# Hybrid attention and convolution step on one core: mixer weights moved to ScalarE's DMA queue, and the convolution's end rewritten

## The chip, the cores and the metric

The kernel runs on one core of a Trainium2 chip. The time is the device time of one execution, in microseconds (us), lower being better. TensorE is written PE, VectorE DVE, ScalarE ACT, GpSimd POOL and SyncE SP, as the profile writes them. The chip runs each engine's instructions in their own order; an instruction that waits holds up what stands behind it on its engine.

## The reference, cut to what matters

One layer of a decoder trunk for 528 prompt tokens (512 and 16 learned ones) and 32 sample tokens (8 sequences of 4), D = 1024, all in float32:

```
h = h + 0.5 * swiglu(rmsnorm(h, ffn1_norm), ffn1_w_gate, ffn1_w_up, ffn1_w_down)
n = rmsnorm(h, mix_norm)
q_lat, q_rope, c_kv, k_rope, glu = project_mixers(n, pos, w_in, q_norm, w_uq, kv_norm, w_uk)
a = attn_fn(q_lat, q_rope, c_kv, k_rope, w_uv)
cv, conv_state = conformer_conv(glu, conv_prev, conv_w, conv_b, conv_ln_g, conv_ln_b)
mix = jnp.concatenate([rmsnorm(a, attn_grp_norm), rmsnorm(cv, conv_grp_norm)], axis=-1) @ w_out
h = h + mix
h = h + 0.5 * swiglu(rmsnorm(h, ffn2_norm), ffn2_w_gate, ffn2_w_up, ffn2_w_down)
```

`conformer_conv` is a causal depthwise convolution of width 31 over 512 channels, then a LayerNorm over the channels and a swish. The sample tokens attend to 4096 cached latent rows each, which lie in pages of 128 rows x 256 columns behind a page table; the prompt attends to itself. After the layer comes a last RMSNorm.

## The kernel before, in words

Tensors lie with channels on the partitions and tokens along the free dimension. The program has three stretches: the first feed-forward part, the mixers (from about 400 to 736 us of the span), and the second feed-forward part with the last norm.

**Weights.** Every float32 weight block of 128x512 (256 KB) is loaded into a `wr` tile (3 of them) by `w_dma` (the DMA is L284, issued by SP), then split by `w_split` into a rounded part `wh` (ACT, L302) and the rest `wl` (POOL, L304). A product takes three matmuls: wh with the high and with the low part of the data, wl with the high part. When block j has been split, the load of block j + 3 is issued; it waits until POOL has read the `wr` tile three blocks back. The mixers' blocks are those of w_in (24), w_r (1), w_uq (4), w_uk (2), w_uv (2) and w_out (16), and `mixers` holds their indices.

**Sample attention.** 32 chunks run one after another, 16 for each of two groups. `load_chunk` issues 8 page DMAs of 256 KB (L1036, SP; tile slots "w" where the chunk's number divides by 3 and is at most LAST_W, otherwise "y", 8 slots, which is two chunks) and 2 indirect DMAs (L1023, POOL). `chunk_scores` gives `sc` (L1070), `chunk_pt` transposes the softmax's numerators into `pts` (L1079, L1081 on ACT), and `chunk_pv` multiplies them with the page (`ob`, L1092); after chunk LAST_W it sets `w_free`, upon which the residual `h` is loaded back (L1588) into the "w" slots.

**Prompt attention.** 16 units in two workers give `s` (L1261), `pr` (L1277), `pts` (L1302), `po` (L1317) and fill `at`.

**Convolution.** `conv_proc` runs 31 taps for each of four channel blocks on DVE (L942) into `acc`. `conv_tail` takes the mean (`mu`), squares the four blocks into four temporaries `sq` of the pool "t", sums the squares over the channels with `rsqrt` (L452, 4 matmuls per block into one PSUM tile `p1`), forms 1/sqrt (L484 is a square root on ACT that needs a table load of its own; L485 to L488 are on DVE), spreads it over the partitions (`spread`, L503 to L507), applies the LayerNorm, the tanh (`th`, L981) and the swish, and does the same again for conv_grp_norm. `scaled` (L900) then writes a temporary `cg`, and `split` (L905 ACT, L906 POOL) makes `conv_out[ct]` of it in a slot of "x" or "z". "z" has 5 slots: two hold the convolution's result `acc2`, two the attention's result `at`.

**The end of the mixers.** `attn_norm` waits for all units and the sample's end, squares `at`, sums, scales in place (L900) and splits into `mix_a` (L905 ACT, L906 DVE), and then gives both slots of `at` back. main() waits for `conv_done` and `w_free`, runs `out_half(conv_out)` eight times (12 matmuls for each half of the tokens, L371) and adds into `h` (L1582); then it waits for the attention's norm and does the same for `mix_a`.

**Order.** The program is written by generators that a planner of its own steps in turn: `yield 0.48` tells how long a step keeps PE, `Sleep(CN_LAT)` how long to stay away, `Ev` is an event. The constants (CN_LAT, AN_LAT, PAGE_LAT ...) are planned latencies, not times of the run. conv_tail and the sample chain have the first priority, the workers the second, main() the last. The PSUM banks are mm 4, sa 2, nr 1, cv 1.

Of the kernel before, what the change touches and what calls it, by code (L numbers as in the profile page):

```python
# [7 lines left out]
F32 = mybir.dt.float32  # L8
F32R = mybir.dt.float32r
I32 = mybir.dt.int32  # L10
AF = mybir.ActivationFunctionType
# [18 lines left out]
NQ = T - META  # L30
# [20 lines left out]
US_LAT = 4.96  # L51
UP_LAT = 0.5
CS_LAT = 1.73
CN_LAT = 8.16
AN_LAT = 3.71
TAP_PACE = 1.05
CN_WAIT = 8.0
# [8 lines left out]
PAGE_LAT = 2.04  # L66
WEIGHT_TIME = 0.0

LAST_W = 30


STEPS = "q0k1plr23ue4567"
# [24 lines left out]
P_CG = 24  # L97
# [14 lines left out]
def kernel(  # L112
# [29 lines left out]
    nc = tc.nc  # L142
# [12 lines left out]
    def U(tag, shape, dt=F32, name="u"):  # L155
        return arena.tile(shape, dt, tag=tag, bufs=slots[tag], name=name)

    def Tm(shape=None, name="t"):
        return tmp.tile(shape or [128, T], F32, tag="t", bufs=10, name=name)
# [21 lines left out]
    def SS(shape, name="ss", who="mm"):  # L181
        return ps_s.tile(shape, F32, tag=BANK_OF[who], bufs=BANKS[BANK_OF[who]], name=name)
# [14 lines left out]
    ones_c = const.tile([128, 128], F32, name="ones_c")  # L197
# [11 lines left out]
    def col(c):  # L209
        return par[:, c:c + 1]  # L210

    def behind(ins, *others):

        for o in others:
            if o is not None:
                tc.add_manual_dep(ins.ins, o.ins.name, mybir.DependencyInfo(
                    mybir.DependencyClass.NoSync, mybir.DependencyReason.DATA), reason="the order in which the products need them")
        return ins


    stream = []
# [22 lines left out]
    mixers = [len(stream)]  # L244
# [9 lines left out]
    mixers = range(mixers[0], len(stream))  # L254
# [16 lines left out]
    def w_dma(upto):  # L271
        while st["dma"] < min(upto, len(subs)):
            i, c0, n = subs[st["dma"]]
            if n == 0:
                if c0 == 0:
                    raws[i, "a"] = []
                    for kh in range(2):
                        t = U("y" if i in first_new else "x", [128, 2, 512], F32, "ra")
                        nc.sync.dma_start(out=t, in_=stream[i][0][:, 1024 * kh:1024 * kh + 1024])
                        raws[i, "a"].append(t)  # L280
                st["dma"] += 1
                continue
            t = wpool.tile([128, n], F32, tag="wr", bufs=3, name="wr")
            nc.sync.dma_start(out=t, in_=stream[i][0][:, c0:c0 + n])  # L284
            raws[st["dma"]] = t
            dma_free[0] = max(dma_free[0], clock[0]) + n * WEIGHT_TIME
            st["dma"] += 1

    def w_split(upto):
        while st["split"] < min(upto, len(subs)):  # L290
            j = st["split"]
            n = subs[j][2]
            w_dma(j + 1)
            if n == 0:
                splits[j] = seven(*subs[j][0:2])
                st["split"] += 1
                w_dma(j + 8)
                continue
            raw = raws.pop(j)
            hi = wpool.tile([128, n], F32R, tag="wh", bufs=3, name="wh")  # L300
            lo = wpool.tile([128, n], F32R, tag="wl", bufs=3, name="wl")
            nc.scalar.activation(out=hi, in_=raw, func=AF.Copy)  # L302
            eng = nc.vector if subs[j][0] in prepared else nc.gpsimd
            eng.tensor_tensor(out=lo, in0=raw, in1=hi.bitcast(F32), op=ALU.subtract)  # L304
            splits[j] = (hi, lo)
            st["split"] += 1

            w_dma(j + (3 if subs[j][0] in mixers else 4))

    def seven(i, m):  # L310
# [133 lines left out]
    last_silu = [None]  # L444
    last_sum = [None]

    def rsqrt(ssums, oi, q, t0=0, site=0, scale=1.0, times=1.0):

        p1 = SS([128, q], "p1", "nr")
        for i, ssum in enumerate(ssums):  # L450
            for j in range(4):
                nc.tensor.matmul(  # L452
                    out=p1[32 * j:32 * j + 32, :], lhsT=ones_c[:, 0:32], rhs=ssum[:, t0 + q * j:t0 + q * j + q],
                    start=(i == 0), stop=(i == len(ssums) - 1), tile_position=(0, 32 * j),
                )
        scale *= (0.5, 2.0, 1.0)[oi]
        r = tmp.tile([128, 3, q], F32, tag="r", bufs=1, name="r")
        r0, r1, rx = (r[:, i] for i in range(3))
        if times != 1.0:
            newton3(p1, r0, r1, rx, scale, times)  # L460
        else:
            newton(p1, r0, r1, scale)

        nc.vector.tensor_copy(out=r1.bitcast(F32R), in_=r0)
        rr = tmp.tile([128, q], F32R, tag="rr", bufs=1, name="rr")
        last_rsqrt[0] = nc.vector.scalar_tensor_tensor(out=rr, in0=r1, scalar=lowm[:, 0:1], in1=r0, op0=ALU.mult, op1=ALU.add)
        return rr
# [51 lines left out]
    def rsqrt_proc(get_ssum, oi, ev, n=NQ, site=0, scale=1.0, times=1.0):  # L519

        q = n // 4
        r0 = rsqrt(get_ssum(), oi, q, 0, site, scale, times)
        yield 0.3
        yield Sleep(RS_LAT)
        rb = tmp.tile([128, n], F32, tag="rb", bufs=2, name="rb")
        spread(rb, r0, site)
        yield 0.95
        ev.set(rb)
# [7 lines left out]
        spawn(norm(), 0)  # L536
        return ev

    def square(part, after=None):
        sq = Tm([128, part.shape[-1]], "sq")  # L540
        behind(nc.scalar.activation(out=sq, in_=part, func=AF.Square), after)
        return sq

# [76 lines left out]
    class Combos:  # L620
# [10 lines left out]
        def split(self, k, names, src, tag, after=None):  # L631
            t = U(tag, [128, 2, src.shape[-1]], F32R, "xc")
            nc.scalar.activation(out=t[:, 0], in_=src, func=AF.Copy)
            behind(nc.vector.tensor_tensor(out=t[:, 1], in0=src, in1=t[:, 0].bitcast(F32), op=ALU.subtract), after)
            for i, name in enumerate(names):
                c = slice(i * self.n, i * self.n + self.n)
                self.at[name, k] = t[:, 0, c], t[:, 1, c]
# [216 lines left out]
    conv_out = [None] * 4  # L854
# [3 lines left out]
    def acc(ct):  # L858
        return acc2[ct // 2][:, ct % 2]
# [38 lines left out]
    def scaled(a, gain, r, out=None):  # L898
        out = a if out is None else out
        nc.vector.scalar_tensor_tensor(out=out, in0=a, scalar=col(gain), in1=r, op0=ALU.mult, op1=ALU.mult)  # L900
        return out
# [57 lines left out]
    def conv_tail():  # L959
        yield Sleep(CS_LAT)  # L960
        for a_ in range(2):
            mu = SS([128, HQ], "mu", ("nr", "cv")[a_])
            nc.tensor.matmul(out=mu, lhsT=ones_c, rhs=csum[0][:, a_ * HQ:a_ * HQ + HQ], start=True, stop=True)
            for ct in range(4):
                a = acc(ct)[:, a_ * HQ:a_ * HQ + HQ]
                nc.vector.tensor_tensor(out=a, in0=a, in1=mu, op=ALU.subtract)
            yield 0.48
            yield Sleep(1.5)
        csum[0] = None
        s = [square(acc(ct)) for ct in range(4)]  # L970
        yield Sleep(CN_LAT)
        ev = Ev()
        yield from rsqrt_proc(lambda: s, 2, ev, site=4)
        s = []
        yield Sleep(1.0)
        for ct in range(4):
            a = acc(ct)
            nc.vector.scalar_tensor_tensor(out=a, in0=a, scalar=col(P_LG + ct), in1=ev.val, op0=ALU.mult, op1=ALU.mult)

            t = Tm([128, NQ], "th")  # L980
            nc.scalar.activation(out=t, in_=a, func=AF.Tanh, scale=0.5, bias=hlb[:, ct:ct + 1])  # L981
            nc.vector.tensor_scalar(out=a, in0=a, scalar1=col(P_LB + ct), scalar2=None, op0=ALU.add)
            nc.vector.scalar_tensor_tensor(out=a, in0=t, scalar=1.0, in1=a, op0=ALU.add, op1=ALU.mult)
            s.append(square(a))
            yield Sleep(0.8)
        yield Sleep(CN_LAT)
        ev = Ev()
        yield from rsqrt_proc(lambda: s, 2, ev, site=5, scale=0.25, times=0.5)
        s = None
        yield Sleep(1.0)  # L990
        for ct in range(4):
            t = scaled(acc(ct), P_CG + ct, ev.val, Tm([128, NQ], "cg"))
            if ct % 2 == 1:
                acc2[ct // 2] = None
            conv_out[ct] = split(t, nc.gpsimd, "x" if ct == 2 else "z")
            yield Sleep(0.8)
        conv_done.set(None, 2.0)

# [17 lines left out]
    def load_chunk(i, after=None):  # L1016
# [3 lines left out]
        rope = small.tile([128, 2, 128], F32, tag="rope", bufs=AHEAD + 1, name="rope")  # L1020
        tiles = [U("w" if i % 3 == 0 and i <= LAST_W else "y", [128, 2, 512], F32, "page") for _ in range(4)]
        for pg in range(2):
# [61 lines left out]
    def chunk_pv(i, pts, al):  # L1084
        g = i // NCHUNK
        _, tiles, _ = chunks.pop(i)
        if i == LAST_W:
            w_free.set(None, 1.0)
# [588 lines left out]
    first = S1("first")  # L1677
# [125 lines left out]
```

## Time and profile before

| what | value |
|---|---|
| runs | 1179.81, 1183.96, 1177.01 us; median 1179.81 |
| profiled execution | 1177.93 us, span 1176.2 us |
| PE busy | 1121.9 us (95% of the span) |
| PE weight loads busy (beside PE) | 1024.0 us |
| DVE / ACT / POOL busy | 779.8 / 536.7 / 333.7 us |
| mean granted TensorE clock | 0.987 |
| chain that ended last | PE 83%, DVE 9%, ACT 3%, DMA 2%, issue 2% |
| DMA queue of SP | 88352 packets, 162.27 MB |
| DMA queue of ACT | 544 packets, 0.56 MB |

The page of the profile cuts the span into 40 slices of 29.4 us. PE stands at 8 or 9 tenths in all but one (the last, with 5), DVE and the DMA engines are high between slices 13 and 24 alone, which is the mixers' stretch; there the DMA share is 0.7 to 0.9 and more. "Idle before" in a row is the time in which that engine stood still just before the instruction, and the arrow names what released it. In a wait of a DMA queue (SPq) the issuing instruction waited, not the transfer.

### The profile page before, as it was taken

To read this page: it belongs to the slowest core of one execution; us is meant where nothing else is said; L and a number is where in the kernel's file an instruction comes from. 1 tells how busy PE (TensorE), PEld (TensorE's weight loads), DVE (VectorE), ACT (ScalarE), POOL (GpSimd) and SP (SyncE) were. 2 spreads that over 40 slices of the span, in tenths; PEclk is the share of its full clock that TensorE was granted. 3 is DMA by queue.
4 is the path that set the end of the run, shared out by engine and by line. 5 is a ranking of instruction groups with operands and counts; after the bars stand their busy time and mean duration, and the time that the engine had idled before them with its cause. 6 is when DMAs were issued, how large, how long until landed. Compare 5 with 4: busy or idle time off the path is not lost.

```text
span 1176.2 us, 24518 instructions
## 1 busy us (share of the span) xinstructions
PE 1121.9 (95%) x9312; PEld 1024.0 (87%) x9312; DVE 779.8 (66%) x1566; ACT 536.7 (46%) x1120; POOL 333.7 (28%) x344
## 2 busy tenths in 40 slices
PE   8999999999999999998889987999999999999995
PEld 8999999999999997876555545999899999999995
DVE  5987158825884447999786457469971698269824
ACT  5555235523565314533544546255552455245631
POOL 4101410042004645676434303342014000410150
PEclk9999999999999999999999999999999999999998
DMA  5243313232226647988889871223333233323222
GB/s 171 70 156 100 90 62 108 88 113 82 92 73 211 223 162 241 267 294 274 232 278 371 309 237 75 77 89 114 102 119 90 61 108 103 100 68 108 68 70 77
DMA packets 91062, 168.60 MB, mean 143 GB/s; under 512 B 18976, under 2 KB 25120, under 8 KB 90944
## 3 DMA queue, kind: packets, MB, share of 16 engines
q1 hardware_dynamic: 88352, 162.27, 42.9%
q0 software_dynamic: 2048, 4.20, 1.2%
q8 instruction: 74, 1.21, 0.4%
q10 hardware_dynamic: 544, 0.56, 0.1%
q14 instruction: 44, 0.36, 0.1%
HBM read 161.33 MB, written 5.65 MB: 142 GB/s over the span
## 4 chain that ended last, share of the span: by engine, by line
PE 83%; DVE 9%; ACT 3%; DMA 2%; issue 2%; POOL 0%; SPq 0%; DVEq 0%; ACTq 0%; POOLq 0%
PE mm L371 39%; PE mm L687 31%; PE sc L1070 3%; DVE cacc L942 2%; PE ob L1092 2%; PE po L1317 2%; PE s L1261 1%; PE mm L1633 1%; PE pt L1301 1%; DMA out<-glu 1%; DVE wl L319 1%; DMA wr<-in_w_in_t 1%; PE p L452 0%; DMA wr<-in_w_out_t 0%; PE pt L1079 0%
## 5 line engine op out<-in xcount | busy, mean ns | idle before, releaser
L687 PE MATMUL mm<-xc,wh 128*128 128x272 f32 (+1 forms) x1960 | 372.8, 290 | 1.5 <-ACT wh L317 1.1
L304 POOL TENSOR_TENSOR wl<-wr,wh 128x512 fp32r<-128x512 f32 (+1 forms) x157 | 198.5, 1268 | 571.4 <-ACT wh L302 504.1
L687 PEld LDWEIGHTS mm<-xc,wh 128*128 128x128 f32 x1960 | 306.4, 188 | 3.0 <-ACT wh L317 2.3
L687 PE MATMUL mm<-xc,wl 128*128 128x272 f32 (+1 forms) x980 | 281.4, 293 | 1.3 <-DVE wl L319 1.3
L371 PE MATMUL mm<-hid,wh 128*128 128x280 f32 (+1 forms) x1352 | 226.8, 289 | 1.8 <-ACT wh L302 1.8
L302 ACT ACTIVATE wh<-wr 128x512 fp32r<-128x512 f32 (+1 forms) x177 | 107.8, 611 | 259.0 <-PE mm L371 192.5
L371 PEld LDWEIGHTS mm<-hid,wh 128*128 128x128 f32 x1352 | 192.5, 188 | 2.0 <-ACT wh L302 2.0
L687 PEld LDWEIGHTS mm<-xc,wl 128*128 128x128 f32 x980 | 182.2, 188 | 7.6 <-DVE wl L319 7.5
L371 PE MATMUL mm<-xs,wh 128*128 128x280 f32 (+2 forms) x992 | 174.5, 295 | 4.1 <-ACT wh L302 1.7
L371 PEld LDWEIGHTS mm<-xs,wh 128*128 128x128 f32 (+1 forms) x992 | 144.6, 189 | 9.0 <-issue 3.5
L807 DVE SCALAR_TENSOR_TENSOR h<-mm,h 128x280 f32<-128x280 f32 (+1 forms) x92 | 36.8, 440 | 166.3 <-PE mm L371 166.3
L371 PE MATMUL mm<-hid,wl 128*128 128x280 f32 (+1 forms) x676 | 141.0, 290 | 0.0
L317 ACT ACTIVATE wh<-ra 128x512 fp32r<-128x512 f32 x140 | 87.5, 629 | 69.6 <-PE mm L687 58.9
L371 PE MATMUL mm<-xs,wl 128*128 128x280 f32 (+2 forms) x496 | 110.6, 297 | 2.3 <-POOL glu L883 1.3
L371 PEld LDWEIGHTS mm<-hid,wl 128*128 128x128 f32 x676 | 106.4, 188 | 0.0
L317 ACT ACTIVATE wh<-ws 128x512 fp32r<-128x512 f32 x105 | 66.2, 630 | 80.2 <-DVE ws L329 41.0
L319 DVE TENSOR_TENSOR wl<-ra,wh 128x512 fp32r<-128x512 f32 x140 | 97.5, 699 | 6.9 <-ACT wh L317 4.2
L942 DVE SCALAR_TENSOR_TENSOR cacc<-glu,par,cacc 128x512 f32<-128x512 f32 x120 | 89.8, 749 | 1.3
L319 DVE TENSOR_TENSOR wl<-ws,wh 128x512 fp32r<-128x512 f32 x105 | 72.4, 690 | 26.9 <-ACT wh L317 24.0
L371 PEld LDWEIGHTS mm<-xs,wl 128*128 128x128 f32 (+1 forms) x496 | 80.4, 189 | 5.1 <-POOL wl L304 1.8
L1023 POOL DMA_INDIRECT rope<-in_pool_r,pr_sb x64 | 62.8, 981 | 47.3 <-PE sc L1070 34.6
L694 ACT ACTIVATE sn<-mm 128x272 f32<-128x272 f32 (+1 forms) x105 | 40.8, 389 | 29.7 <-PE mm L687 29.6
(252 smaller groups left out, 1491.3 us busy)
## 6 DMA issues: line engine op xcount, KB each, us to landing
page<-in_pool_c SPq DMA_DIRECT2D x256, 256.0 KB
ra<-in_f_gu SPq DMA_DIRECT2D x70, 512.0 KB
wr<-in_f_d SPq DMA_DIRECT2D x62, 256.0 KB
wr<-in_f_gu SPq DMA_DIRECT2D x36, 256.0 KB
wr<-in_w_in_t SPq DMA_DIRECT2D x24, 256.0 KB
wr<-in_f_d SPq DMA_DIRECT2D x30, 192.0 KB
wr<-in_w_out_t SPq DMA_DIRECT2D x16, 256.0 KB
h<-in_x_t SPq DMA_DIRECT2D x8, 280.0 KB
```

Source lines behind the costliest of these rows:

```text
L302: nc.scalar.activation(out=hi, in_=raw, func=AF.Copy)
L304: eng.tensor_tensor(out=lo, in0=raw, in1=hi.bitcast(F32), op=ALU.subtract)
L317: nc.scalar.activation(out=hi, in_=w, func=AF.Copy)
L319: ins = nc.vector.tensor_tensor(out=lo, in0=w, in1=hi.bitcast(F32), op=ALU.subtract)
L371: nc.tensor.matmul(out=ps[a][:m, 0:n], lhsT=w, rhs=x[:, a * n:(a + 1) * n], start=first and o == 0 and j == 0, stop=last and o == 1,)
L687: nc.tensor.matmul(out=ps, lhsT=w_[:, c], rhs=x, start=first and k == 0 and j == 0, stop=k == 3 and j == 2, skip_group_check=True)
L694: nc.scalar.activation(out=s, in_=src, func=AF.Copy)
L807: last = halves(lambda o, i, x: nc.vector.scalar_tensor_tensor(out=o, in0=i, scalar=0.5, in1=x, op0=ALU.mult, op1=ALU.add), hk(d), ps, hk( ...
L942: last_tap = nc.vector.scalar_tensor_tensor(out=ps, in0=g[:, tp:S0 + tp], scalar=w, in1=ps, op0=ALU.mult, op1=ALU.add)
L1023: last = nc.gpsimd.indirect_dma_start(out=rope[:, pg], out_offset=None, in_=pool_r, in_offset=bass.IndirectOffsetOnAxis(ap=pr_sb[:, 32 * g ...
L1070: nc.tensor.matmul(out=ps[32 * b:32 * b + 32], lhsT=w[:, g, 32 * b:32 * b + 32], rhs=x, start=(i_ == 0), stop=(i_ == 2), tile_position=(0, ...
L1092: nc.tensor.matmul(out=ob[32 * b:32 * b + 32, :], lhsT=pts[:, 128 * pg + 32 * b:128 * pg + 32 * b + 32], rhs=tiles[b][:, pg, 0:256], start ...
```

## The change

Three things change. The weight loads of the mixers are issued from ACT's queue in place of SP's. conv_tail writes each square into a slot of "g" (the slots of the convolution's input, free after the taps) and sums it into a PSUM tile at once, four matmuls per block, with planned latencies SQ_LAT and SW_LAT in place of CN_LAT; the tanh's temporary lies in "g" too and takes the second square; the last scaling is done in place, without `cg`, and an `acc2` slot is given back after the split that reads it. LAST_W is 27 in place of 30, so that chunk 30's pages go to "y" and `w_free` is set after chunk 27.

```diff
-CN_LAT = 8.16
+SQ_LAT = 1.2
+SW_LAT = 3.4
...
-LAST_W = 30
+LAST_W = 27
...
-            nc.sync.dma_start(out=t, in_=stream[i][0][:, c0:c0 + n])
+            (nc.scalar if i in mixers else nc.sync).dma_start(out=t, in_=stream[i][0][:, c0:c0 + n])
...
+    def column_sums(p1, ssum, q, first, last, t0=0):
+        for j in range(4):
+            nc.tensor.matmul(
+                out=p1[32 * j:32 * j + 32, :], lhsT=ones_c[:, 0:32], rhs=ssum[:, t0 + q * j:t0 + q * j + q],
+                start=first, stop=last, tile_position=(0, 32 * j),
+            )
...
-        s = [square(acc(ct)) for ct in range(4)]
-        yield Sleep(CN_LAT)
+        p1 = SS([128, NQ // 4], "p1", "nr")
+        for ct in range(4):
+            sq = square(acc(ct), None, "g")
+            yield Sleep(SQ_LAT)
+            column_sums(p1, sq, NQ // 4, ct == 0, ct == 3)
+            sq = None
+            yield 0.25
...
-            t = Tm([128, NQ], "th")
+            t = U("g", [128, NQ], F32, "th")
...
-            s.append(square(a))
-            yield Sleep(0.8)
-        yield Sleep(CN_LAT)
+            nc.scalar.activation(out=t, in_=a, func=AF.Square)
+            yield Sleep(SW_LAT)
+            column_sums(p1, t, NQ // 4, ct == 0, ct == 3)
+            t = None
+            yield 0.25
...
-            t = scaled(acc(ct), P_CG + ct, ev.val, Tm([128, NQ], "cg"))
+            conv_out[ct] = split(scaled(acc(ct), P_CG + ct, ev.val), nc.gpsimd, "x" if ct == 2 else "z")
             if ct % 2 == 1:
                 acc2[ct // 2] = None
-            conv_out[ct] = split(t, nc.gpsimd, "x" if ct == 2 else "z")
             yield Sleep(0.8)
```

How this moves the instructions is shown at three places.

The first is ACT's order around chunk 8, before and then now. `r` is the square root of a norm, `p,lb` the numerators of chunk 8, `pts` the transposed ones that PE waits for, `wh` a split of a weight block.

```order
L541 ACTIVATE sq<-cc 128x560 x2
L1081 ACTIVATE pts<-pt 128x256
L302 ACTIVATE wh<-wr 128x512
L484 ACT_TABLE_LOAD
L484 ACTIVATE r<-p_6963,epsb 128x140
L1051 ACT_TABLE_LOAD
L1051 ACTIVATE p,lb<-sc,nm 128x256
L1055 ACTIVATE al<-nm 128x1
```

```order
L548 ACTIVATE sq<-cc 128x560 x2
L1095 ACTIVATE pts<-pt 128x256
L304 ACTIVATE wh<-wr 128x512
L286 DMA wr<-in_w_in_t 128x512 [waits DMAHW5_49,Pool_49]
L286 DMA wr<-in_w_in_t 128x512 [waits DMAHW0_49,Pool_49]
L491 ACT_TABLE_LOAD
L491 ACTIVATE r<-p_6963,epsb 128x140 [waits PE_49]
L1065 ACT_TABLE_LOAD
L1065 ACTIVATE p,lb<-sc,nm 128x256 [waits DVE_49]
L1069 ACTIVATE al<-nm 128x1
```

Two weight loads now stand between a split and the square root, and each waits for POOL and for an earlier transfer.

The second is SP's order at the end of the pages, before and then now: `page` are the page loads, `h<-hscr` the four loads of the residual, `wuv` a weight that the sample's end needs.

```order
L1036 DMA page<-in_pool_c 128x512
L1181 DMA wuv<-in_w_uv_t 128x1024
L1588 DMA h<-hscr 128x1088 x4
L284 DMA wr<-in_w_out_t 128x512 x10
L284 DMA wr<-in_f_gu 128x512 x14
```

```order
L1602 DMA h<-hscr 128x1088 [waits DMAHW4_49,PE_49]
L1045 TENSOR_LOAD pg_sb
L1050 ISA
L1050 DMA page<-in_pool_c 128x512 [waits DMAHW5_49,PE_49]
L1050 ISA
L1050 DMA page<-in_pool_c 128x512 [waits DMAHW6_49,PE_49]
```

The four loads of `h`, behind all pages before, now stand after 30 of the 32 chunks, and the 16 page loads of chunks 30 and 31 behind them.

The third is the end of the mixers. First PE's order from the last `ob` (the sample's last chunk) to the spread of the attention's norm, before and then now. `p<-sq` sums squares, `p<-rr` spreads a norm, `mm<-mix` is the output projection.

```order
L1092 MATMUL ob<-page,pts 32x256 x8
L452 MATMUL p_9703<-sq,ones_c 32x136 x4
L1132 MATMUL ot<-cst,o_acc_91 128x128 x2
...
L452 MATMUL p_9769<-sq,ones_c 32x136 x16
L371 MATMUL mm<-mix,wh 128x272 x6
L371 MATMUL mm<-mix,wl 128x272 x2
...
L503 MATMUL p_9816<-rr,unit 128x136
```

```order
L1106 MATMUL ob<-page,pts 32x256 x8
L1331 MATMUL po<-pr,vt 64x128 x2
L372 MATMUL mm<-mix,wh 128x272 x2
L372 MATMUL mm<-mix,wl 128x272
L1146 MATMUL ot<-cst,o_acc_91 128x128 x2
...
L450 MATMUL p_9773<-sq,ones_c 32x136 x8
L372 MATMUL mm<-mix,wh 128x272 x2
L372 MATMUL mm<-mix,wl 128x272
L450 MATMUL p_9773<-sq,ones_c 32x136 x8
L510 MATMUL p_9824<-rr,unit 128x136
```

Then ACT's order of the splits there, now, with the tiles' numbers: `acc_5750` and `acc_7309` are the two halves of `acc2`, `at_7978` and `at_8811` those of `at`, and mix_9766, 9770, 9800 and 9804 the four convolution parts 0 to 3.

```order
L912 ACTIVATE mix_9766<-acc_5750 128x544 [waits DVE_49]
L912 ACTIVATE mix_9800<-acc_7309 128x544 [waits DVE_49]
...
L912 ACTIVATE mix_9837<-at_7978 128x544 [waits DMAHW6_49,DMAHW2_49,DVE_49]
L912 ACTIVATE mix_9841<-at_7978 128x544 [waits DMAHW5_49,DMAHW7_49,DMAHW3_49,DVE_49]
L912 ACTIVATE mix_9845<-at_8811 128x544 [waits DMAHW4_49,DMAHW5_49,DMAHW0_49,DVE_49]
L912 ACTIVATE mix_9849<-at_8811 128x544 [waits DMAHW5_49,DMAHW1_49,DVE_49]
L912 ACTIVATE mix_9770<-acc_5750 128x544 [waits DVE_49]
L912 ACTIVATE mix_9804<-acc_7309 128x544 [waits DVE_49]
```

The convolution's sums no longer lie between the last `ob` and the attention's sums. Of the convolution's half of the projection (192 matmuls) 12 stand ahead of the spread, where 35 stood before, and none between the attention's last sums and the spread. Parts 1 and 3 of the convolution, mix_9770 and mix_9804, are split behind the attention's four parts, where before all four (from `cg`) came ahead of them.

## Rows read from the trace of the kernel before

**Rows 1.** Windows: PE, PEld, DVE, ACT, POOL busy (instructions), clock, DMA share, GB/s.

```profile
500.00:540.00 40.00, 36.35 (x359) 30.62 (x352) 38.10 (x67) 14.73 (x33) 30.05 (x29) 1.00 0.84 271
540.00:580.00 40.00, 32.15 (x263) 22.68 (x265) 34.45 (x70) 19.49 (x53) 20.37 (x23) 0.95 0.88 280
...
722.00:736.00 14.00, 7.56 (x60) 6.39 (x52) 12.55 (x16) 7.77 (x14) 9.87 (x6) 1.00 0.06 19
```

**Rows 2.** Timeline of PE, long stalls: start, length, instruction, [idle before <-releaser].

```profile
535.48 0.33 PE L503 MATMUL p<-rr,unit 2*128 2x140 f32 x1 [1.17 <-ACT rb L505]
...
579.25 1.07 PE L1070 MATMUL sc<-rope,qbd 128*32 128x256 f32 x8 [4.41 <-ACT pts L1081]
...
678.51 1.93 PE L1092 MATMUL ob<-page,pts 128*32 128x256 f32 x16 [3.27 <-ACT pts L1081]
```

**Rows 3.** Timelines of SP and ACT: weight loads and the splits that wait for them.

```profile
514.17 0.34 SPq L284 DMA_DIRECT2D wr<-in_w_in_t  x1
...
516.92 0.63 ACT L302 ACTIVATE wh<-wr 128x512 fp32r<-128x512 f32 x1 [1.82 <-DMA wr<-in_w_in_t]
...
572.55 7.70 SPq L284 DMA_DIRECT2D wr<-in_w_out_t  x4
...
577.93 0.63 ACT L302 ACTIVATE wh<-wr 128x512 fp32r<-128x512 f32 x1 [4.24 <-DMA wr<-in_w_out_t]
```

**Rows 4.** Waits of SP's queue, 380 to 780 us: in total, times, longest.

```profile
SPq L284 <- POOL wl L304: 105.9, 34, 28.0
SPq L1036 <- PE ob L1092: 26.8, 11, 6.3
```

**Rows 5.** Timelines of ACT, DVE and POOL around chunk 8.

```profile
509.58 0.63 ACT L302 ACTIVATE wh<-wr 128x512 fp32r<-128x512 f32 x1 [1.06 <-issue]
...
512.66 0.38 ACT L484 ACTIVATE r<-p,epsb 128x140 f32<-128x140 f32 x1 [1.15 <-PE p L452]
...
514.15 1.28 POOL L304 TENSOR_TENSOR wl<-wr,wh 128x512 fp32r<-128x512 f32 x1
```

**Rows 6.** Timelines of SP and PE at the end of the pages.

```profile
690.10 2.78 SPq L1036 DMA_DIRECT2D page<-in_pool_c  x5
...
687.31 1.07 PE L1092 MATMUL ob<-page,pts 128*32 128x256 f32 x16
...
696.73 1.07 PE L1092 MATMUL ob<-page,pts 128*32 128x256 f32 x16 [0.53 <-ACT pts L1081]
697.62 0.61 PE L1070 MATMUL sc<-rope,qbd 128*32 128x256 f32 x8
...
703.51 0.61 PE L1070 MATMUL sc<-rope,qbd 128*32 128x256 f32 x8
...
708.47 1.07 PE L1092 MATMUL ob<-page,pts 128*32 128x256 f32 x16
```

**Rows 7.** Timeline of PE at the end of the mixers.

```profile
721.08 1.14 PE L452 MATMUL p<-sq,ones_c 128*32 128x136 f32 x32 [0.42 <-DVE rb L507]
...
729.89 0.34 PE L503 MATMUL p<-rr,unit 2*128 2x136 f32 x4 [0.85 <-DVE rr L466]
...
736.22 0.75 PE L371 MATMUL mm<-mix,wh 128*128 128x272 f32 x2 [4.17 <-DVE h L1582]
...
742.35 0.67 PE L371 MATMUL mm<-mix,wh 128*128 128x272 f32 x4
...
743.10 0.67 PE L371 MATMUL mm<-mix,wh 128*128 128x272 f32 x4
```

**Rows 8.** Timelines of ACT, DVE and POOL there: square root, scalings, splits.

```profile
725.33 0.37 ACT L484 ACTIVATE r<-p,epsb 128x136 f32<-128x136 f32 x1
...
730.91 4.90 DVE L900 SCALAR_TENSOR_TENSOR at<-at,par,rb 128x544 f32<-128x544 f32 x4
...
737.12 2.62 DVE L906 TENSOR_TENSOR mix<-at,mix 128x544 fp32r<-128x544 f32 x4
...
722.71 6.31 POOL L906 TENSOR_TENSOR mix<-cg,mix 128x544 fp32r<-128x544 f32 x4 [8.58 <-ACT mix L905]
```

More of the change, by code (lines that the diff above doesn't have):

```diff
@@ L445 @@
     last_sum = [None]
-    def rsqrt(ssums, oi, q, t0=0, site=0, scale=1.0, times=1.0):
[L449 to L455, printed above, removed]
+    def column_sums(p1, ssum, q, first, last, t0=0):
[4 more added lines that the diff above has]
+            )
+    def rsqrt(ssums, oi, q, t0=0, site=0, scale=1.0, times=1.0):
+        if isinstance(ssums, list):
+            p1 = SS([128, q], "p1", "nr")
+            for i, ssum in enumerate(ssums):
+                column_sums(p1, ssum, q, i == 0, i == len(ssums) - 1, t0)
+        else:
+            p1 = ssums
         scale *= (0.5, 2.0, 1.0)[oi]
@@ L537, in rsqrt_after, with square @@
         return ev
-    def square(part, after=None):
-        sq = Tm([128, part.shape[-1]], "sq")
+    def square(part, after=None, home="t"):
+        sq = Tm([128, part.shape[-1]], "sq") if home == "t" else U(home, [128, part.shape[-1]], F32, "sq")
         behind(nc.scalar.activation(out=sq, in_=part, func=AF.Square), after)
@@ L969, in conv_tail @@
         csum[0] = None
-        s = [square(acc(ct)) for ct in range(4)]
-        yield Sleep(CN_LAT)
+        p1 = SS([128, NQ // 4], "p1", "nr")
[5 more added lines that the diff above has]
+            yield 0.25
         ev = Ev()
-        yield from rsqrt_proc(lambda: s, 2, ev, site=4)
-        s = []
+        yield from rsqrt_proc(lambda: p1, 2, ev, site=4)
+        p1 = None
         yield Sleep(1.0)
+        p1 = SS([128, NQ // 4], "p1", "nr")
         for ct in range(4):
@@ L983, in conv_tail @@
             nc.vector.scalar_tensor_tensor(out=a, in0=t, scalar=1.0, in1=a, op0=ALU.add, op1=ALU.mult)
-            s.append(square(a))
-            yield Sleep(0.8)
-        yield Sleep(CN_LAT)
+            nc.scalar.activation(out=t, in_=a, func=AF.Square)
[3 more added lines that the diff above has]
+            yield 0.25
         ev = Ev()
-        yield from rsqrt_proc(lambda: s, 2, ev, site=5, scale=0.25, times=0.5)
-        s = None
+        yield from rsqrt_proc(lambda: p1, 2, ev, site=5, scale=0.25, times=0.5)
+        p1 = None
         yield Sleep(1.0)
         for ct in range(4):
-            t = scaled(acc(ct), P_CG + ct, ev.val, Tm([128, NQ], "cg"))
+            conv_out[ct] = split(scaled(acc(ct), P_CG + ct, ev.val), nc.gpsimd, "x" if ct == 2 else "z")
             if ct % 2 == 1:
                 acc2[ct // 2] = None
-            conv_out[ct] = split(t, nc.gpsimd, "x" if ct == 2 else "z")
             yield Sleep(0.8)
```

## The prediction, as it was put on record

> **What bounds the kernel now.** The page of the profile comes first: PE is busy 95% of the span and holds 83% of the chain that ended last, so a change pays only where PE stands still. The windows then show where that is. In the feed-forward stretches PE has next to no gap, while in the mixers it loses 3.65 us of the 40 from 500 to 540, 7.85 of the next 40, and 6.44 of the 14 us from 722 to 736 [rows 1]. Third, the timeline of PE names what ended the long gaps: 1.17 us at 535 and 4.41 us at 579, both behind ACT, and 3.27 us at 678, behind ACT again [rows 2]. ACT's own timeline says what it stood for. At 577.93 its split had waited 4.24 us for a weight load of which the first was issued at 572.55, that is 5.38 us before; the `pts` that PE needed stood behind that split [rows 3]. The gap at 678 has no transfer in it: ACT loads the square root's table, takes the root and loads the exponential's table.
>
> The waits of SP's queue tell whether the weight loads hold the pages up. SP stood long for weights (its loads wait for POOL), but the page loads themselves waited 26.8 us for `ob`, the multiplication that gives their slots back [rows 4]. So taking weights out of SP's order lets few pages go earlier: the next one still waits for `ob`.
>
> The end of the mixers is a chain of its own. The attention's sums start at 721.08, the spread at 729.89, and from 736.22 on PE runs the rest of the projection without a gap [rows 7].
>
> **The change, part by part.** *Weight loads on ACT, the waits that go.* Pages no longer stand ahead of a weight load on its queue. A load with little ahead of it, issued at 514.17, released its split at 516.92, 2.75 us later, against 5.38 [rows 3]. If that holds, the 4.41 us shrink by 5.38 − 2.75 = 2.63, and the 1.17 us go: **−3.8**. At most both go, −5.6; at least nothing.
>
> The Trainium skill ("DMA: Bandwidth & Descriptors", section "Issuing engines are not separate DMA queues") says the contrary: DMAs of all engines run on the same 16 DMA engines, and a second issuing engine saves the issuing time alone. By that the term is 0 and the sum 3.8 us higher. The transfers in the mixers do already fill 0.84 to 0.88 of those engines [rows 1], so the rule has the trace's load on its side; the 2.75 us speak against it only as far as that load met a free queue.
>
> *Weight loads on ACT, the waits that come.* Each of 48 loads now stands in ACT's order and waits for POOL's split three blocks back. The worst place is chunk 8. The split ahead of the two loads ended at 509.58 + 0.63 = 510.2, and POOL's second `wl` at 514.15 + 1.28 = 515.4 [rows 5]: ACT would stand 5.2 us. The root behind it ran at 512.66 and would run at about 516 to 517. Behind that are the exponential and `pts` of chunk 8, on which PE waits; DVE is busy 38.10 of 40 us there and can't make up for a late norm [rows 1]. PE has projection work to fill in, with 3.65 us of gaps in 40. So between 0 (PE goes on with projections) and 5 us, and I take **+2**, nearer to the fill. The other places come to 0.5 us each, off the path; they are kept for the range.
>
> *LAST_W 27.* The pages of chunks 30 and 31 now wait for the `ob` of chunks 28 and 29, and stand behind the four loads of `h`. Before, the last pages were issued from 690.10 to 692.88, after the `ob` of 687.31 [rows 6]. Now chunk 31's come after 696.73 + 1.07 = 697.8. A chunk is 8 x 0.262 = 2.1 MB, 7.5 us at the 280 GB/s of [rows 1], so its pages land at about 705.3, against the 703.51 of its `sc`: 1.8 us late. PE has workers' steps moved into that place (next term), so I take **0**, the upper end being 8 us if `h` (2.2 MB, 8 us at that rate) delays both chunks in full.
>
> *The convolution's end, its sums and roots.* The number of matmuls, squares and roots stays. Both norms of the convolution now lie among the pages, at chunks 23 to 28 by the order. The stall of 3.27 us [rows 2] moves with the first norm; the second norm's root, before in the end, now meets the sample's chain too. Between 0 and another 3.3 us; **+1**, since the chain is the only thing it meets there and workers' steps fill most of it.
>
> *The end of the mixers.* What is late next is the convolution's half of the projection. "z" has five slots: two `acc2`, two `at`, one for part 0. Scaling in place keeps `acc2` until part 1 is split, and part 1 needs a slot that only `at` gives back; before, `cg` held the scaled values and `acc2` was free. The order shows it: part 1 is split behind the attention's parts. So:
> - From the last `ob` (708.47 + 1.07 = 709.5) to the end of the attention's sums there is less to do, some 7.5 us in place of 12.7, by what the order leaves there.
> - From the sums' end to the spread PE has nothing (before, 35 matmuls): table load, then root to spread, 729.89 − 725.33 = 4.6 us [rows 7, 8], with 0.7 us ahead: 5.3 us.
> - From the spread, scalings begin after 730.91 − 729.89 = 1.0 us and take 4.90; then two splits on DVE (2.62 / 4 = 0.66 each) free the slot, and ACT needs 0.65: 7.9 us. POOL's half takes 6.31 / 4 = 1.58 [rows 8], so PE goes on without a gap at about 9.5 us after the spread.
> - Then 176 matmuls at (743.10 − 742.35) / 6 = 0.125 us [rows 7]: 22.0 us.
>
> From the last `ob` that is 7.5 + 5.3 + 9.5 + 22.0 = 44.3 us. Before it was 736.22 − 709.5 = 26.7 and 144 matmuls, 18.0: 44.7. Counted so, −0.4. But the workers' steps that left the end stand ahead of the last `ob` now, where PE was all but full, so the better count is of PE's idle time: before 0.42 and 6.44 us [rows 1, 7], now 5.3 and 8.6 (9.5 less the few matmuls in it). That is +7.0. The moved steps, some 5 us, are hidden as far as the gaps ahead of `ob` (those of the last pages, above) take them in; by half. I take **+4**, between −0.4 and +7.0.
>
> **The sum:** −3.8 + 2 + 0 + 1 + 4 = +3.2. On the profiled execution (1177.93 us, of which 1.7 lie around the span) that is 1181.1; the median of the three runs is 1179.81, 1.9 us above it, so 1183.0 us.
>
> **The rivals.** *ACT held by its own loads (slower).* At chunk 8 the full 5.2 us reach PE, 1.6 us at a `pts` of chunk 11 and 0.5 us at some eight other loads ahead of a `pts`: 10.8 in place of 2, so 1191.8. For it: ACT's order is fixed and `pts` has no slack, as 4.41 us show. Against: POOL may reach its splits earlier, as loads land earlier. It decides from the point where ACT stands longer for POOL than PE has projections to run.
>
> *The moved work fills gaps (faster).* Both waits for weights go (−5.6), ACT isn't held, no second stall, and all moved steps are hidden (−0.4): −6.0, so 1173.8. For it: between 540 and 580 PE lost 7.85 us, more than these. Against: the block on "z".
>
> *The weights land no earlier.* The loads share the engines with the pages whichever queue they come from, and ACT's splits wait as before: 0 in place of −3.8, so 1186.8. For it: the DMA share of 0.84 to 0.88. Against: the time of 5.38 us is mostly a place behind pages issued earlier. This is the skill's rule, above.
>
> **How the numbers follow.** The forecast has a chance of 0.40, ACT held 0.18, the moved work 0.24, the late weights 0.18. What a measurement of this kernel can tell from no change is about 0.5%, 5.9 us: faster is below 1173.9, slower above 1185.7. The faster rival lies at that border and reaches to 1169 with the small gaps that it may fill besides; I count 0.20 of its 0.24 and 0.03 of the forecast as faster: 0.23. Slower are all of ACT held, half of the late weights, and 0.10 of the forecast (its upper end, with 8 us for the last pages): 0.37. The rest, 0.40, is no change that can be told. The range goes from 1169 to 1193, from the faster rival's lower end to just above the slower one.
>
> **What would show it.** In the profile after: no wait of ACT's `wh` for a weight load above 3 us in the mixers (above 4, the late weights are right); waits of ACT's queue for POOL of several us around chunk 8 and a `pts` of PE behind them; `ob` still the releaser of the page loads; at the end, a PE gap of about 5 us ahead of the spread, and one of 7 to 8 us behind it, released by ACT's split of part 1. Should PE run projections through both, the count of "z" is wrong, and with it the +4. A total below 1173 or above 1190 would make the prediction wrong.

## The result, and the profile after

The changed kernel ran at a median of 1186.01 us (1180.35 to 1190.32, 20 runs) against 1181.03 us (1177.01 to 1188.35, 20 runs): a ratio of 1.0051 with a 95% interval of 1.0035 to 1.0066. It is half a per cent slower, 5 to 6 us, inside the range and on the side of the forecast (+3.2 us). The profiled execution took 1184.39 us, its span 1182.6 us against 1176.2.

PE was busy 1127.9 us in place of 1121.9, with the same 9312 matmuls, and so idle 54.7 us in place of 54.3. The idle time only changed its place: the gaps that the change took away came back elsewhere, and the same matmuls together ran 6.0 us longer. In this pair the mean granted clock differs too, 0.987 before and 0.981 now; group 2 of the experiments below compares the two kernels at the same mean clock. First the windows that answer to [rows 1], with three larger ones (columns as there):

```profile
500.00:540.00 40.00, 36.08 (x365) 29.32 (x363) 36.22 (x62) 15.68 (x37) 31.40 (x31) 1.00 0.89 281
540.00:580.00 40.00, 35.96 (x302) 26.45 (x302) 38.11 (x82) 20.87 (x58) 23.34 (x25) 0.99 0.94 287
722.00:736.00 14.00, 4.82 (x88) 3.60 (x86) 7.80 (x16) 7.35 (x15) 0.00 (x0) 0.76 0.01 1
...
460.00:580.00 120.00, 110.88 (x1025) 86.73 (x1027) 109.15 (x204) 51.32 (x132) 73.93 (x74) 1.00 0.90 285
580.00:690.00 110.00, 99.32 (x1054) 54.45 (x1050) 81.61 (x253) 56.49 (x189) 47.32 (x76) 0.95 0.89 309
690.00:745.00 55.00, 43.96 (x416) 28.23 (x409) 21.43 (x68) 23.98 (x70) 6.06 (x12) 0.86 0.26 87
```

The same three large windows of the kernel before:

```profile
460.00:580.00 120.00, 107.82 (x1013) 85.71 (x1015) 110.06 (x201) 51.85 (x131) 73.26 (x74) 0.98 0.89 282
580.00:690.00 110.00, 99.99 (x1043) 56.06 (x1036) 68.69 (x228) 51.90 (x186) 43.13 (x74) 0.97 0.89 308
690.00:745.00 55.00, 45.64 (x477) 32.68 (x476) 38.45 (x101) 29.10 (x76) 14.36 (x17) 0.97 0.30 103
```

From 460 to 580 PE lost 9.1 us in place of 12.2: the first part of the change paid 3.1 us. From 690 to 745 it lost 11.0 in place of 9.4, and the granted clock fell from 0.97 to 0.86. PE's timeline of the changed kernel names the gaps, those of [rows 2] and those of [rows 7]:

```profile
578.99 1.08 PE L1084 MATMUL sc<-rope,qbd 128*32 128x256 f32 x8 [0.47 <-ACT pts L1095]
...
725.66 0.67 PE L450 MATMUL p<-sq,ones_c 128*32 128x136 f32 x16
730.32 0.48 PE L510 MATMUL p<-rr,unit 2*128 2x136 f32 x4 [3.99 <-DVE rr L473]
736.38 1.27 PE L372 MATMUL mm<-mix,wh 128*128 128x272 f32 x4 [5.57 <-ACT mix L912]
738.16 0.82 PE L372 MATMUL mm<-mix,wh 128*128 128x272 f32 x2 [0.51 <-POOL mix L913]
...
739.24 1.11 PE L372 MATMUL mm<-mix,wh 128*128 128x272 f32 x4
...
740.60 1.11 PE L372 MATMUL mm<-mix,wh 128*128 128x272 f32 x4
```

The gap of 4.41 us at chunk 14 is 0.47. At the end, PE stands 3.99 us ahead of the spread and 5.57 behind it, the second released by ACT's split of a convolution part, `mix`, as the count of the "z" slots said. ACT's timeline shows that split, and that it waited for DVE's split of an attention part:

```profile
735.67 0.66 ACT L912 ACTIVATE mix<-acc 128x544 fp32r<-128x544 f32 x1 [0.61 <-DVE mix L913]
```

Six matmuls then take 740.60 − 739.24 = 1.36 us, 0.227 each, in place of the 0.125 of [rows 7]. Those rows begin 6 us behind the gap of the kernel before. Right behind that gap its matmuls were as slow: three take 737.67 − 736.99 = 0.68 us, 0.227 each. PE's timeline of the kernel before, and under it its windows (columns as above), in which the granted clock falls to 0.57 behind the gap and is 1.00 again from 740 on:

```profile
736.99 0.66 PE L371 MATMUL mm<-mix,wh 128*128 128x272 f32 x2
...
737.67 0.66 PE L371 MATMUL mm<-mix,wh 128*128 128x272 f32 x2
```

```profile
732.00:736.00 4.00, 0.05 (x1) 0.00 (x0) 4.00 (x4) 2.27 (x5) 3.22 (x2) 1.00 0.20 66
736.00:740.00 4.00, 3.79 (x18) 3.79 (x19) 4.00 (x9) 0.50 (x1) 0.00 (x0) 0.57 0.22 70
740.00:744.00 4.00, 4.00 (x35) 4.00 (x34) 0.60 (x3) 0.77 (x2) 1.28 (x1) 1.00 0.02 4
```

Two marks settle where the 6.4 us of the span lie. The rest of the projection began at 736.38 against 736.22: up to there these two executions are level. From there to the end the changed one needs 1182.6 − 736.38 = 446.2 us, the other 1176.2 − 736.22 = 440.0. Of the convolution's 192 matmuls 12 were done by then in place of 48, so 180 − 144 = 36 more were left over, which are 4.5 of these 6.2 us; another 0.51 is the wait for POOL, and the last 1.2 go with the low clock, which lasts longer here than in the kernel before.

The second part of this reading holds in every profile with a gap behind the spread: from the mark to the end the kernels with the new end of the convolution need 446.2 to 447.4 us (the changed kernel, 1b, 2a, 2c, 2d, 3a, 3d below), those with the old one 440.0 to 442.6 (the kernel before, 1a, 1c, 2b, 3c). The first part does not: the mark itself moves between executions of one kernel, to 742.65 in 2a and 735.18 in 3a, both the changed kernel.

### The profile page after: what moved, and what is told of

The parts are those of the page before. It is cut to its first block, busy times and chain, and to the rows that moved or that the text cites. A ratio compares the mean times of both kernels' runs of the same rounds, so it can differ in the third digit from the quotient of the medians.

```text
span 1182.6 us, 24514 instructions
## 1 busy us (share of the span) xinstructions
PE 1127.9 (95%) x9312; PEld 1024.2 (87%) x9312; DVE 772.8 (65%) x1566; ACT 537.4 (45%) x1120; POOL 334.7 (28%) x344
## 4 chain that ended last, share of the span: by engine, by line
PE 82%; DVE 7%; DMA 3%; ACT 3%; issue 2%; POOL 1%; SPq 0%; ACTq 0%; DVEq 0%; POOLq 0%
PE mm L372 39%; PE mm L694 31%; PE sc L1084 3%; DMA page<-in_pool_c 3%; PE ob L1106 2%; PE po L1331 1%; PE s L1275 1%; PE mm L1647 1%; DVE cacc L949 1%; PE pt L1315 1%; DVE wl L320 1%; PE v L1252 1%; DMA rope<-in_pool_r,pr_sb 1%; POOL wl L306 0%; PE p L450 0%
```

## The experiments

The runs were made in three groups of four kernels, each group on one chip, with runs of the kernel before between them (its medians: 1187.65, 1181.77 and 1181.16 us). The interval is that of the ratio to it.

| run | weights on | end | LAST_W | median us | ratio | interval |
|---|---|---|---|---|---|---|
| 1a | ACT | old | 30 | 1180.53 | 0.9950 | 0.9923 to 0.9976 |
| 1b | SP | new | 30 | 1182.70 | 0.9952 | 0.9925 to 0.9980 |
| 1c | SP | old | 27 | 1186.99 | 1.0006 | 0.9980 to 1.0033 |
| 1d | ACT | new, `cg` in g | 27 | 1176.24 | 0.9916 | 0.9885 to 0.9946 |
| 2a (the changed kernel) | ACT | new | 27 | 1186.83 | 1.0046 | 1.0027 to 1.0065 |
| 2b (the kernel before) | SP | old | 30 | 1180.74 | 0.9995 | 0.9975 to 1.0016 |
| 2c | ACT | new | 30 | 1183.84 | 1.0015 | 0.9994 to 1.0035 |
| 2d | SP | new | 27 | 1187.09 | 1.0042 | 1.0019 to 1.0064 |
| 3a (the changed kernel) | ACT | new | 27 | 1184.94 | 1.0028 | 1.0012 to 1.0045 |
| 3b | ACT | new, `cg` in g | 27 | 1172.52 | 0.9929 | 0.9903 to 0.9956 |
| 3c | ACT | old | 30 | 1178.81 | 0.9973 | 0.9948 to 0.9998 |
| 3d | SP | new | 30 | 1179.89 | 0.9979 | 0.9960 to 0.9999 |

### The parts alone (1a, 1b, 1c)

**1a, weights on ACT:**

```diff
-            nc.sync.dma_start(out=t, in_=stream[i][0][:, c0:c0 + n])
+            (nc.scalar if i in mixers else nc.sync).dma_start(out=t, in_=stream[i][0][:, c0:c0 + n])
```

> The kernel before with the mixers' weight loads issued from ACT, nothing else. Theory (the end's slots cost the time): about 2 us below the kernel before (-3.8 for the two waits that go, +2 for ACT's stand at chunk 8), so a ratio of 0.996 to 1.000; the gap of 4.41 us at chunk 14 is gone, ACT still stands about 5 us for POOL ahead of a square root, and the end (gaps of 0.85 us ahead of the spread and 4.17 us behind it) is that of the kernel before. Rival (ACT held by its own loads costs the time): 5 us or more above the kernel before, ratio 1.004 or more.

It came out at 0.9950, and at 0.9973 in the repeat 3c: faster, by a little more than expected the first time. The waits of ACT in 1a, 460 to 580 us, have the stand at chunk 8 (L484 is the table load ahead of the root):

```profile
ACT L484 <- POOL wl L304: 6.2, 1, 6.2
```

PE's timeline of 1a shows what is left of the stall at chunk 14:

```profile
579.69 0.64 PE L1070 MATMUL sc<-rope,qbd 128*32 128x256 f32 x8 [0.47 <-ACT pts L1081]
```

ACT does stand 6.2 us for POOL, and the kernel is faster all the same. The rival, that ACT's own loads cost the time, falls. Seven kernels with the loads on ACT (the changed kernel, 1a, 2a, 2c, 3a, 3b, 3c) have 0.47 us in that place, each in a profile of its own; the kernel before has 4.41 and, in 2b, 3.34.

**1b, the new end of the convolution**, the changed kernel with two lines put back:

```diff
-LAST_W = 27
+LAST_W = 30
...
-            (nc.scalar if i in mixers else nc.sync).dma_start(out=t, in_=stream[i][0][:, c0:c0 + n])
+            nc.sync.dma_start(out=t, in_=stream[i][0][:, c0:c0 + n])
```

> The kernel before with the new conv_tail alone: weights on SP, LAST_W 30. Theory: PE stands 4 us ahead of the attention's spread and 5 to 6 us behind it, and with the wait for weights at chunk 14 kept the time is 5 to 9 us above the kernel before, ratio 1.004 to 1.008. Rival (ACT held): no slower than the kernel before, ratio 0.998 to 1.002, since ACT issues no load.

A miss. It gave 0.9952, and 0.9979 in the repeat 3d, where 1.004 to 1.008 was expected, though the gaps are all there. PE's timeline of 3d:

```profile
580.01 1.08 PE L1084 MATMUL sc<-rope,qbd 128*32 128x256 f32 x8 [3.72 <-ACT pts L1095]
...
698.48 0.62 PE L1084 MATMUL sc<-rope,qbd 128*32 128x256 f32 x8
...
725.32 0.34 PE L510 MATMUL p<-rr,unit 2*128 2x136 f32 x4 [3.27 <-DVE rr L473]
731.22 1.28 PE L372 MATMUL mm<-mix,wh 128*128 128x272 f32 x4 [5.57 <-ACT mix L912]
733.01 0.82 PE L372 MATMUL mm<-mix,wh 128*128 128x272 f32 x2 [0.51 <-POOL mix L913]
```

PE's timeline of 1b, from chunk 30's scores to the spread:

```profile
702.42 0.61 PE L1084 MATMUL sc<-rope,qbd 128*32 128x256 f32 x8
...
729.21 0.34 PE L510 MATMUL p<-rr,unit 2*128 2x136 f32 x4 [3.27 <-DVE rr L473]
```

From chunk 30's scores to the spread it is 26.8 us in both, where it was 729.89 − 697.62 = 32.3 [rows 6, 7]: 5.5 us of steps have left this stretch. They stand ahead of it now, and did not push it back by their full length: the spread comes 4.6 us earlier than the 729.89 of the kernel before in 3d, though only 0.7 us in 1b. Against that stand 36 matmuls more behind the gaps, 4.5 us. Single executions cannot tell how far the two cancel; by the ratios the new end by itself is no loss.

**1c, LAST_W alone**, one constant:

```diff
-LAST_W = 30
+LAST_W = 27
```

> The kernel before with LAST_W 27 in place of 30, nothing else. Theory: within 2 us of the kernel before, the pages of chunk 31 some 2 us late with other work of PE to cover them. Rival (the late pages cost the time): chunk 31's scores 5 us or more later than before and the time 4 to 7 us above it, ratio 1.003 to 1.006.

1.0006, with 0.9980 to 1.0033: no change, as the theory said. The first half of the rival came true all the same, as PE's timeline of 1c shows (chunks 30 and 31):

```profile
698.27 0.61 PE L1070 MATMUL sc<-rope,qbd 128*32 128x256 f32 x8
...
708.49 0.61 PE L1070 MATMUL sc<-rope,qbd 128*32 128x256 f32 x8
```

Chunk 31's scores come 10.2 us after chunk 30's in place of 703.51 − 697.62 = 5.9 [rows 6], and 5.0 us later than before. They cost nothing that can be told here.

### Do the parts add up (2a to 2d)

The first two parts alone looked faster and the whole slower, in another group of runs, so the second group put the whole and two pairs side by side.

> The changed kernel as it is, beside the parts on one chip. If the parts interact (theory 1: the late pages of LAST_W 27 cost once the conv's end lies among the pages), it stands 4 to 6 us above the kernel before, ratio 1.003 to 1.006, though two of its parts alone gave 0.995. If the difference lies with the chip and its granted clock (theory 2), it stands at or below the kernel before, ratio 0.992 to 0.999.

> The kernel before as it is, as a control with a profile of its own on the chip of these runs: ratio 1.000 within 0.003 by both theories. By theory 2 its granted clock is lower than the 0.987 of the first profile, and the stretches at the lower level lie elsewhere or are more.

```diff
-LAST_W = 27
+LAST_W = 30
```

> The changed kernel with LAST_W 30: weights on ACT and the new end of the convolution. Theory 1: the two gains of the parts alone add up, ratio 0.988 to 0.993. Theory 2: within 0.2% of the changed kernel of the same call.

```diff
-            (nc.scalar if i in mixers else nc.sync).dma_start(out=t, in_=stream[i][0][:, c0:c0 + n])
+            nc.sync.dma_start(out=t, in_=stream[i][0][:, c0:c0 + n])
```

> The changed kernel with the weight loads back on SP: the new end of the convolution and LAST_W 27. Theory 1: the gain of the end alone (0.995) is lost to late pages, ratio 1.002 to 1.007, the scores of chunk 31 some 7 us later than in the run with the end alone. Theory 2: 0.993 to 0.999, as the end alone.

The control 2b gave 0.9995, and the kernel before ran in this group at a mean granted clock of 0.980. The changed kernel is slower here too, 1.0046, at that same mean clock of 0.980, and so is the new end with LAST_W 27 on SP (2d, 1.0042). Both parts without LAST_W 27 (2c) are at 1.0015, not to be told from no change. So theory 2 falls as far as the changed kernel goes, and theory 1 holds in half: with the new end, LAST_W 27 comes out 3.0 us slower (1186.83 against 1183.84, their intervals overlap), but the two gains do not add up to 0.988 to 0.993.

The late scores show in PE's timeline, 2c first (chunks 30 and 31):

```profile
704.33 0.64 PE L1084 MATMUL sc<-rope,qbd 128*32 128x256 f32 x8
...
711.63 0.61 PE L1084 MATMUL sc<-rope,qbd 128*32 128x256 f32 x8
```

and 2a, the changed kernel:

```profile
704.58 0.64 PE L1084 MATMUL sc<-rope,qbd 128*32 128x256 f32 x8
...
716.89 0.61 PE L1084 MATMUL sc<-rope,qbd 128*32 128x256 f32 x8
```

Chunk 31 follows chunk 30 after 12.3 us in place of 7.3. In 2d, for which 7 us were expected, it is 11.5 us, 4.1 more than in 3d. Yet PE's longest gap in that place of 2a is 0.67 us, behind ACT and not behind a page. So the 5 us are workers' steps that the program's order puts ahead of chunk 31, not a wait for pages; from chunk 30's scores to the attention's spread it is 32.0 us in place of 28.9 (spreads at 736.60 and 733.21). The late pages of theory 1 were not seen, only their planned place. That place alone is not the cost either: 1c has a like delay without a loss, and so has 3b below, the fastest kernel (chunk 31 at 711.89, 12.3 us after chunk 30). The slower kernels with LAST_W 27 (2a, 2d, 3a) all have the new end's gaps as well. Why the two cost together was not tried by an edit of its own and stays open.

### The slots of "z" (1d, 3a, 3b)

The cause of the gap behind the spread is tried by one edit of the changed kernel: the scaled values go to a slot of "g", as they went to `cg` before, and `acc2` is free ahead of the split.

```diff
-            conv_out[ct] = split(scaled(acc(ct), P_CG + ct, ev.val), nc.gpsimd, "x" if ct == 2 else "z")
+            t = scaled(acc(ct), P_CG + ct, ev.val, U("g", [128, NQ], F32, "cg"))
             if ct % 2 == 1:
                 acc2[ct // 2] = None
+            conv_out[ct] = split(t, nc.gpsimd, "x" if ct == 2 else "z")
+            t = None
```

> The changed kernel with the last scaling written to a temporary in a slot of g, so that acc2 goes back before parts 1 and 3 are split and they no longer wait for the attention's slots. Theory: the gaps of 3.99 and 5.57 us around the spread are filled with projections, and 5 to 9 us go: 0.5% to 0.8% below the changed kernel, at or a little below the kernel before (ratio to it 0.997 to 1.001). Rivals (ACT held; late pages): the gaps close but the time stays within 2 us of the changed kernel, ratio to the kernel before 1.004 to 1.006.

The first time it gave 0.9916, more than expected, but without the changed kernel on that chip. The third group has both.

> The changed kernel once more, to stand beside the next three on one chip. Ratio to the kernel before 1.003 to 1.007 if the two earlier results hold on every chip; 0.994 to 0.999 if the chip of the first four experiments, on which the kernel before was 6 us slower than elsewhere, is one on which the order of the two turns round and this is that chip.

> The changed kernel with the scaled convolution in a temporary of g, beside the changed kernel on one chip. Theory (the slots of z hold up the projections): 8 to 12 us below the changed kernel, 0.7% to 1.0%, since 9.6 us of gaps around the spread close and the matmuls behind them run at the full clock. Rival (the last result was the chip's): within 0.3% of the changed kernel.

> Weights on ACT alone, once more. Theory (worth its 3 us of gaps between 460 and 580, less what is lost later): ratio to the kernel before 0.997 to 1.001, and 4 to 7 us below the changed kernel. Rival (ACT held): at the changed kernel's time or above it.

> The new end of the convolution alone, once more. Theory: ratio to the kernel before 1.000 to 1.005, the gaps at the spread (3 and 5.6 us) against fewer steps elsewhere. Rival (the end is a gain of 0.5%, as the first result read): 0.993 to 0.997.

Of these, 3a came out at 1.0028, just under what was expected. 3c, at 0.9973, is 6.1 us below the changed kernel, as expected. 3d missed again, at 0.9979 in place of 1.000 to 1.005, and its rival's 0.993 to 0.997 missed too.

3b took 1172.52 us against 1184.94 for the changed kernel: 12.4 us or 1.0% less, a little above what the theory expected, and 0.71% below the kernel before. Windows of the changed kernel's first profile, of 4 us each, and under them those of 3b:

```profile
728.00:732.00 4.00, 0.48 (x4) 0.29 (x4) 3.03 (x9) 0.46 (x2) 0.00 (x0) 0.64 0.00 0
732.00:736.00 4.00, 0.00 (x0) 0.00 (x0) 4.00 (x7) 2.96 (x5) 0.00 (x0) 0.50 0.00 0
736.00:740.00 4.00, 3.11 (x12) 2.79 (x13) 0.91 (x2) 0.98 (x2) 3.00 (x2) 0.50 0.00 0
740.00:744.00 4.00, 4.00 (x24) 4.00 (x24) 0.20 (x1) 0.33 (x1) 0.00 (x0) 0.65 0.00 0
```

```profile
728.00:732.00 4.00, 4.00 (x43) 3.28 (x40) 0.54 (x2) 1.56 (x3) 0.00 (x1) 1.00 0.00 0
732.00:736.00 4.00, 4.00 (x34) 4.00 (x34) 2.77 (x6) 2.02 (x3) 1.92 (x2) 1.00 0.22 67
736.00:740.00 4.00, 4.00 (x34) 3.78 (x34) 3.55 (x9) 1.09 (x3) 1.94 (x2) 1.00 0.22 71
740.00:744.00 4.00, 4.00 (x34) 4.00 (x33) 4.00 (x8) 2.94 (x5) 1.66 (x1) 1.00 0.26 66
```

In 3b PE has no gap in the whole end: from 690 to 745 it is idle 0.8 us in place of 11.0 (the changed kernel's first profile, and 3a). It runs 34 matmuls in 4 us at a granted clock of 1.00, where the changed kernel, its projections once begun, runs 24 at 0.65. So the slots of "z" cost more than the two gaps (9.6 us). The rest, 2.8 us, fits the clock: the mean granted clock of the runs is 0.985 in 3b and 0.982 in 3a, which at the 0.9 us per thousandth of the last section is an estimate of some 3 us. The clock was not varied by itself. 3b is also the fastest kernel of its group, ahead of both that were compared.

## Why the prediction was right, step by step

- **The number alone decides nothing.** 1186.01 us lies 3.0 above the forecast of 1183.0, just over its border for "slower", 1185.7, and nearest to the rival "the weights land no earlier" with 1186.8. The runs speak against that rival: the loads on ACT alone are no slower (1a, 3c), and the wait that it would keep is gone.
- **What bounds the kernel** held: the changes that the profiles show lie in PE's gaps and in its clock.
- **The waits for weights that go, −3.8.** The size came near and half of the reason was wrong. The gaps of 1.17 and 4.41 us shrank to nothing and 0.47, and PE's idle time from 460 to 580 by 3.1 us (by 1.0 in the pair 2b and 2a, from 9.8 to 8.8). The first half of the reason held: pages no longer stand ahead of a weight load. But the loads do not land faster on ACT's queue. For the kernel before, the trace holds no landing of a `wr` load. 3d and 3c, on one chip, have it for a part of the loads from 440 to 600 us; the view of that tile gives for SP's queue (3d) and then for ACT's (3c):

```profile
DMA to landing us min/median/max: 2.5/5.4/7.5
...
DMA to landing us min/median/max: 2.6/5.5/8.3
```

The forecast had set 2.75 against 5.38 from issue to split. What the Trainium skill says ("DMA: Bandwidth & Descriptors", section "Issuing engines are not separate DMA queues"), that DMAs of all engines run on the same 16 DMA engines, agrees with these two medians. Its other half, that the saving is the time of issuing alone and usually small, does not fit this case: SP's order also holds page loads, and they wait for other things. SP's timeline of the kernel before, just ahead of that weight load, has eight of them; from 555 to 575 the issues of pages waited 5.5 us in all, for PE and for earlier transfers. ACT's timeline, under it, shows the load of the projection's weights issued at 568.19, where SP came to it at 572.55 [rows 3]:

```profile
565.04 7.41 SPq L1036 DMA_DIRECT2D page<-in_pool_c  x8
...
568.19 2.64 ACTq L286 DMA_DIRECT2D wr<-in_w_out_t  x2
...
575.63 0.63 ACT L304 ACTIVATE wh<-wr 128x512 fp32r<-128x512 f32 x1 [0.64 <-DMA wr<-in_w_out_t]
```

The rival "the weights land no earlier" was right on the transfer and wrong on the wait: the split waited 0.64 us in place of 4.24.

- **The waits that come, +2.** The stand was foreseen, its price was too high. ACT's timeline at chunk 8:

```profile
518.69 1.62 ACTq L286 DMA_DIRECT2D wr<-in_w_in_t  x2
520.34 1.28 ACT L491 ACT_TABLE_LOAD   x1 [5.22 <-POOL wl L306]
521.63 0.38 ACT L491 ACTIVATE r<-p,epsb 128x140 f32<-128x140 f32 x1
```

5.22 us against 5.2; the same stand is 5.0 to 6.2 us in 1a, 2a, 2c, 3a and 3c. PE ran projections meanwhile: in the 40 us from 500 to 540 it lost 3.92 us in place of 3.65. Of the signs listed beside it, one failed by its letter. ACT's splits waited for weight loads 8.1 us in all from 400 to 740, in place of 21.7, but one wait, for `w_r` at 436.68, was 4.07 us. By the sign that speaks for the late weights, but PE had no gap there, and 2a and 3a have no such wait.

- **LAST_W, 0.** Right alone (1.0006). With the new end it was about 3 us, and no late page was seen there.
- **The second square root, +1.** From 580 to 690 PE lost 10.7 us in place of 10.0: +0.7 (in 2a and 2b 10.3 and 9.1). The 3.27 us at one place became gaps of 1.7 us and less.
- **The end, +4.** The mechanism was right: part 1 is split behind the attention's parts, and PE stands ahead of the spread and behind it. The gaps were put too long, 5.3 and 8.6 us in place of 3.99 and 5.57 + 0.51. Two sizes failed: the four scalings took 2.87 us and not 4.90, and the last two steps of the root on DVE 0.30 each and not 0.62 and 1.34 (those were the times of the kernel before, with POOL at work beside them). One term was missing on both sides of the sum, the clock behind a gap: all matmuls were counted at 0.125 us, while the first ones behind the gap took 0.227 in both kernels. Of the 6.2 us lost from 736 on, the longer low clock has up to 1.2 (6.2 − 4.5 − 0.51). The kernel before paid a part of the same price, which fits 3b, without the gaps, being faster than both.

The sum is so right by parts that went astray both ways. The half that I took for the moved steps could not be measured: with the end alone the spread comes 0.7 us (1b) or 4.6 us (3d) earlier than before, and in three profiles of the changed kernel it lies at 729.13, 730.32 and 736.60. How the parts take the gain from each other (0.9973 and 0.9979 alone, 1.0015 together, on two chips) is not settled: the differences are near the width of the intervals. That the sum came out so near the measured time is luck; the block on "z" is not.

## What to carry to other kernels

When a temporary is saved by working in place, look up who waits for the slot that is now held longer: here one saved temporary held two blocks of a projection behind an unrelated norm, and one slot elsewhere gave 1.0% back. A DMA moved to a second queue gains what its old neighbours in the issuing order cost it, not transfer time. Judge a new gap of PE with the matmuls behind it, for they may run at half the clock.

## What the runs showed of the hardware that was not expected

The spread between runs of one kernel goes with PE's clock. In the first group the kernel before took 1177.69 us at a mean granted clock of 0.989 and 1190.34 us at 0.975: 12.65 us for 14 thousandths, 0.9 us each, where a thousandth of 1180 us is 1.2. The clock was read beside the time, not set. Runs of one kernel differ by as much as these kernels do from each other, so only many runs on one chip, side by side, told them apart.

Behind the gap of the changed kernel the granted clock was 0.50, which is the lower of its two levels, 1.2 GHz, while PE stood still from 732 to 736 and while it worked from 736 to 740. The kernel before, with a gap of 4.17 us, has 0.57 from 736 to 740, and its matmuls there were as slow; in 3b, where PE did not pause, it stayed at 1.00, the 2.4 GHz.

DVE's work on whole tiles took longer where POOL worked beside it. The four scalings of the kernel before are in [rows 8], 4.90 us from 730.91 on; POOL split weights beside them, the first row below. In the changed kernel (the next two rows) POOL starts only at 736.41, behind them, and in 3b (the last row) it stands still for most of them:

```profile
731.67 3.55 POOL L304 TENSOR_TENSOR wl<-wr,wh 128x512 fp32r<-128x512 f32 x2 [2.65 <-ACT wh L302]
...
731.49 2.87 DVE L907 SCALAR_TENSOR_TENSOR at<-at,par,rb 128x544 f32<-128x544 f32 x4
...
736.41 3.00 POOL L913 TENSOR_TENSOR mix<-acc,mix 128x544 fp32r<-128x544 f32 x2 [22.00 <-ACT mix L912]
...
739.45 2.93 DVE L907 SCALAR_TENSOR_TENSOR at<-at,par,rb 128x544 f32<-128x544 f32 x4
```

0.72 us each in place of 1.22, for the same operation on the same shapes. Transfers are not the difference: in the windows with the scalings 3b moved 66 to 71 GB/s, and the kernel before 66 in the one from 732 on. That POOL is the reason was not tried by itself.
